# Delta-rule values and two gated branch outputs transposed on VectorE and through DRAM instead of on TensorE

## The chip, the cores and the metric

The kernel runs on one core of a Trainium2 chip. Its engines are TensorE (PE for its matmuls, PEld for its weight loads), VectorE (DVE), ScalarE (ACT), GpSimd (POOL) and SyncE (SP); each takes its own instructions in the order in which they were put into its queue. The metric is the device time of one execution in microseconds (us). A profiled execution gives the trace; its own time and its span (first to last instruction) are told beside the times of unprofiled runs.

## What is computed

One decoder layer on 256 tokens of width 2048, in float32. A token mixer adds three gated branches (multi-head latent attention, MLA; gated linear attention, GLA; gated DeltaNet, GDN); a convolutional gated MLP follows. What the change touches:

```python
h = rms_norm(x, attn_norm)
(..., gla_r, gdn_qkv, ..., gdn_z, merge) = split(h @ w_in)
# gated DeltaNet, chunks of the delta rule: 8 value heads of 128
v = silu(causal_dwconv(gdn_qkv, conv_w))[values]
u0 = triangular_solve(t_mat, beta * v)
...
y_gdn = rms_norm(o_gdn) * gain * silu(gdn_z)        # (256, 1024)
y_gla = rms_norm(o_gla) * gain * silu(gla_r)        # (256, 1024), 4 heads of 256
mixed = g_mla * (y_mla @ w_branch_mla) + g_gla * (y_gla @ w_branch_gla) + g_gdn * (y_gdn @ w_branch_gdn)
x = x + mixed @ w_out
x = x + conv_ffn(rms_norm(x))
return rms_norm(x, final_norm)
```

## The kernel before

Every large product keeps float32 accuracy by splitting both operands into a rounded high part and a low remainder. A weight piece of 128x1024 is loaded by SP (`raw`), rounded by ScalarE (`hi`, L191) and subtracted by VectorE (`lo`, whose operation shows as L103). There are four buffers each of `raw`, `hi` and `lo`, so a piece can be split ahead of its use. `t_chunk` (L237 to L239) gives 512 columns with tokens on the partitions, in matmuls of 128x512. `fj_chunk` (L212, L213) gives features on the partitions. Helpers record their own line: L103 is every elementwise product or sum, L106 every scalar-tensor-tensor operation, L293 the gain of `gained`.

A left operand of `t_chunk` must have features on the partitions. So a result with tokens on the partitions is transposed before it is a left operand again. There are two ways in the kernel. `gated_out` and V's scaling transpose 128x128 blocks on TensorE against an identity matrix, into PSUM. `turned` lets VectorE transpose inside 32x32 blocks (L304), writes the result to DRAM through POOL's queue (L306) and reads it back with the blocks in place, in four transfers per pair of 128-column blocks (L312); `gained_sb` then applies the gain and splits (ScalarE L323, VectorE L106). `turned` serves the merged sum and x + mixer, in three of their four chunks of 512 columns each.

The stages around the change, by the profile: the MLA branch until about 208 us; GDN's convolutions and gates until 265; its 31-step triangular solve on VectorE, 276 to 318, whose result POOL writes to DRAM and reads back (L759, L768); GDN's matmuls L796 to L832 until 435; GLA's projections q, k (an F chunk), V (`lv`, L944) and gate until 559; four GLA heads (L1026 and on) from 580 to 682. Merges (gate columns times branch product) and GDN's and GLA's projections lie between these on TensorE. `merge(0, y_mla)` fills the GDN stage; `merge(2, y_gdn, c)` is written after each GLA head; `merge(1, y_gla, c)` follows the heads.

Three places matter. V: `gv`, four tiles with two blocks of 128 features by 256 tokens each, is transposed at L781 (16 transposes) and multiplied by `vs` into `vt`, which L811 uses. GDN output: `gated_out` scales `o_gdn`, transposes (L865, 16) and splits into `hi_y` and `lo_y`. GLA output: the same function, 16 more transposes at L865, into `hi_E` and `lo_E`.

The order of each engine's queue is not written by hand: a planner simulates the program with its own costs for instructions and transfers, and takes what is ready by program order. An instruction can be tied behind the one written before it on its engine (`keep_in_program_order`). SBUF is handed out by tags with a fixed number of buffers (`S(tag)`); the tags of one region take the bytes of the region closed before it, tile by tile. In the GDN region those tags include "hq" (8 buffers) and "t" (4); in the GLA region "lqkv" (12), "E" (8) and "t" (4).

Of the kernel before, what the change touches and what calls it, by code (L numbers as in the profile page):

```python
# [9 lines left out]
F32 = mybir.dt.float32  # L10
# [3 lines left out]
AF = mybir.ActivationFunctionType  # L14
# [41 lines left out]
def trunk(ctx, tc, A, out, dbg=None, stop=None):  # L56
# [4 lines left out]
    def nm(s):  # L61
        serial[0] += 1
        return f"{s}{serial[0]}"
# [18 lines left out]
    def S(tag, shape=(P, 512), dt=F32, n=None):  # L82
        p, bufs = pools[tag]
        return p.tile(list(shape), dt, name=nm(n or tag), tag=tag, bufs=bufs)

    def PS(n="ps"):
        return pp.tile([P, 512], F32, name=nm(n), tag="mix")
# [7 lines left out]
    def keep(shape, n, dt=F32):  # L95
        return cp.tile(list(shape), dt, name=n)
# [5 lines left out]
    def tt(o, a, b, op, eng=None):  # L102
        (eng or dve).tensor_tensor(o, a, b, op=op)  # L103

    def stt(o, a, s, b, op0, op1):
        dve.scalar_tensor_tensor(o, a, s, b, op0=op0, op1=op1)  # L106
# [179 lines left out]
    def gained(psb, gains, store):  # L286

        hi, lo = store.new()
        if not isinstance(store, Joint):
            hi, lo = ([v[:, j] for j in range(2)] for v in (hi, lo))  # L290
        for j, g in enumerate(gains):
            src = psb[:, j * 256:(j + 1) * 256]
            act.activation(hi[j], src, AF.Copy, scale=g)  # L293
            stt(lo[j], src, g, hi[j], MUL, SUB)

    def turned(src, tags, n=512):

        nk = n // P  # L300
        d = dp.tile([2 * P, n], F32, name=nm("d_t"))
        for t in range(2):
            v = S(tags[0], (P, n), n="tr")
            dve.transpose(v.rearrange("p (b k i) -> p k b i", b=4, k=nk),  # L304
                          src[t].rearrange("p (k b i) -> p k b i", b=4, k=nk))
            pool.dma_start(d[t * P:(t + 1) * P], v)  # L306
        dv = d.rearrange("(a j) (b k i) -> b j a k i", j=32, b=4, k=nk)
        res = []
        for g in range(nk // 2):
            r = S(tags[1], (P, 8, 2, 32), n="rd")  # L310
            for b in range(4):
                pool.dma_start(r[b * 32:(b + 1) * 32], dv[b, :, :, 2 * g:2 * g + 2])  # L312
            res.append(r)
        return res

    def gained_sb(r, gains, store):

        hi, lo = store.new()
        if not isinstance(store, Joint):
            hi, lo = ([v[:, j] for j in range(2)] for v in (hi, lo))  # L320
        for j, g in enumerate(gains):
            h_, l_ = (v[j].rearrange("p (a i) -> p a i", i=32) for v in (hi, lo))
            act.activation(h_, r[:, :, j], AF.Copy, scale=g)  # L323
            stt(l_, r[:, :, j], g, h_, MUL, SUB)


    def row_stats(tiles, n):
# [307 lines left out]
        stt(gdec[:, t, :], xg[:, t, :], -1.0, ea, MUL, MUL)  # L635


    sel = keep([P, 68], "sel", F32R)
    pool.memset(sel.bitcast(F32), 0.0)
    pool.memset(sel[:, 3:4].bitcast(F32), 1.0)  # L640
# [133 lines left out]
    for gp in ((0, 1), (2, 3)):  # L774

        vts = {}
        for g in gp:
            psb = PS().rearrange("p (t x) -> p t x", t=2)
            for a in range(2):
                for t in range(2):  # L780
                    pe.transpose(psb[:, t, a * P:(a + 1) * P], gvv[2 * g + a][:, t * P:(t + 1) * P], ident)  # L781
            vts[g] = S("vt", (P, 2, 2, P))
            tt(vts[g].rearrange("p t a d -> p t (a d)"), psb, vs[:, :, g:g + 1].to_broadcast([P, 2, 256]), MUL)
        for s in (32, 64):
            work = []
            Pms = {g: S("Pm", (P, 4, s), n="Pm") for g in gp}
            for p in range(64 // s):
                for g in gp:
                    b1, b2 = slice(2 * p * s, 2 * p * s + s), slice(2 * p * s + s, 2 * p * s + 2 * s)
                    psb = PS()  # L790
                    pv = [psb[:, k * 128:k * 128 + 4 * s].rearrange("p (u j) -> p u j", u=4) for k in
                          ((0, 1, 2) if s == 32 else (0, 2))]
                    work.append((b1, b2, pv, Pms[g], Ms[g], Ys[g], Xs[g]))
            for b1, b2, pv, Pm, M, Y, X in work:
                for u in range(4):
                    pe.matmul(pv[0][b2, u, :], M[b1, u, b2], X[b1, u, b1], start=True, stop=True, **sk)  # L796
                dve.tensor_copy(Pm[b2], pv[0][b2])
            for b1, b2, pv, Pm, M, Y, X in work:
                for u in range(4):
                    pe.matmul(pv[1][b1, u, :], Pm[b2, u, :], Y[b2, u, b2], start=True, stop=True, **sk)  # L800
                dve.tensor_scalar(Y[b1, :, b2], pv[1][b1], -1.0, None, op0=MUL)
            if s == 32:
                for b1, b2, pv, Pm, M, Y, X in work:
                    for u in range(4):
                        pe.matmul(pv[2][b2, u, :], Y[b2, u, b2], Pm[b2, u, :], start=True, stop=True, **sk)
                    dve.tensor_scalar(X[b2, :, b1], pv[2][b2], -1.0, None, op0=MUL)
        u0s, W0s, R1s, W1s = {}, {}, {}, {}
        for g in gp:
            u0s[g] = PS()
            for a in range(2):  # L810
                pe.matmul(u0s[g][:, a * P:(a + 1) * P], Ys[g][:, a * 2, :], vts[g][:, 0, a, :], start=True, stop=True)  # L811
            W0s[g] = S("w", (P, 2, P), n="W0")
            tt(W0s[g], u0s[g][:, :256].rearrange("p (a d) -> p a d", a=2), b3(wj[:, 0, 2 * g:2 * g + 2], P), MUL)
        for g in gp:
            for a in range(2):
                pe.matmul(u0s[g][:, 256 + a * P:256 + (a + 1) * P], hqs[g][1][:, 1, a, :], W0s[g][:, a, :],
                          start=True, stop=True)
            R1s[g] = S("w", (P, 2, P), n="R1")
            tt(R1s[g], vts[g][:, 1], u0s[g][:, 256:].rearrange("p (a d) -> p a d", a=2), SUB)
        for g in gp:  # L820
            u1 = PS()
            for a in range(2):
                pe.matmul(u1[:, a * P:(a + 1) * P], Ys[g][:, a * 2 + 1, :], R1s[g][:, a, :], start=True, stop=True)
            W1s[g] = S("w", (P, 2, P), n="W1")
            tt(W1s[g], u1[:, :256].rearrange("p (a d) -> p a d", a=2), b3(wj[:, 1, 2 * g:2 * g + 2], P), MUL)
        for g in gp:
            op = PS().rearrange("p (t a d) -> p t a d", t=2, a=2)
            q0, q1 = hqs[g]
            for a in range(2):
                pe.matmul(op[:, 0, a, :], q0[:, 0, a, :], W0s[g][:, a, :], start=True, stop=True)  # L830
                pe.matmul(op[:, 1, a, :], q0[:, 1, a, :], W0s[g][:, a, :], start=True, stop=False)
                pe.matmul(op[:, 1, a, :], q1[:, 0, a, :], W1s[g][:, a, :], start=False, stop=True)  # L832
            os_ = S("d", (P, 2, 2, P), n="og")
            dve.tensor_copy(os_, op)
            o_gdn.append(os_)
            for a in range(2):
                for t in range(2):
                    junk = S("t", (P, P), n="junk")
                    c = t * 8 + 2 * g + a
                    act.activation(junk, os_[:, t, a, :], AF.Square, accum_out=gst[:, c:c + 1])  # L840
# [12 lines left out]
    for t in range(2):  # L853
        dve.tensor_scalar(fg[:, t, :], fg[:, t, :], rx[:, t:t + 1], None, op0=MUL)

    def gated_out(o_tiles, f_of, zs, gcol, name, ytag):

        y = Act(8, ytag)
        for g in range(4):
            o = o_tiles[g]  # L860
            f_of(g, o, [zs[t][g // 2][:, (g % 2) * 256:(g % 2) * 256 + 256] for t in range(2)])
            psb = PS()
            for a in range(2):
                for t in range(2):
                    pe.transpose(psb[:, a * 256 + t * P:a * 256 + (t + 1) * P], o[:, t, a, :], ident)  # L865
            gained(psb, [half_gain[:, gcol + 2 * g + a:gcol + 2 * g + a + 1] for a in range(2)], y)
            if dbg is not None and ("y_" + name) in dbg:
                full = S("t", (P, 2, 256), n="dbg")
                tt(full, y.hi[g].bitcast(F32), y.lo[g], ADD)
                sync.dma_start(dbg["y_" + name][:, 2 * g:2 * g + 2, :], full)  # L870
        return y

    def gates_of(c0, name, tag):
# [49 lines left out]
            tt(ov, ov, z[t], MUL)  # L923
        tt(o, o, fg[:, :, 2 * g:2 * g + 2].unsqueeze(3).to_broadcast([P, 2, 2, P]), MUL)

    y_gdn = gated_out(o_gdn, scale_gdn, zs, 8, "gdn", "y")
    if stop == "gdn":
        return

# [11 lines left out]
    for c in range(2):  # L941
        for t, bank in enumerate(t_chunk(w_in, GLA_V + c * 512, ht)):
            lv[t][c] = [S("lqkv", dt=F32R, n="lv") for _ in range(2)]
            act.activation(lv[t][c][0], bank, AF.Copy, scale=rx[:, t:t + 1])  # L944
            stt(lv[t][c][1], bank, rx[:, t:t + 1], lv[t][c][0], MUL, SUB)

    sr = gates_of(GLA_R, "rs", "d")


# [117 lines left out]
            ov = o[:, t].rearrange("p a d -> p (a d)")  # L1067
            stt(ov, ov, fl8[:, 2 * g + t:2 * g + t + 1], z[t], MUL, MUL)

    y_gla = gated_out(o_gla, scale_gla, sr, 0, "gla", "E")  # L1070
    if stop == "gla":
        return

# [206 lines left out]
```

## Time and profile before

| what | value |
|---|---|
| median of 3 runs | 1671.26 us (1670.92 to 1671.31) |
| profiled execution | 1671.5 us, span 1669.7 us, granted TensorE clock 0.998 |
| PE busy, PEld busy | 1656.2 us, 1406.8 us, 9068 instructions each |
| DVE busy | 1106.4 us, 1740 instructions |
| ACT busy | 828.0 us, 1157 instructions |
| POOL busy | 135.7 us, 202 instructions |
| DMA | 314.96 MB, mean 189 GB/s |

How to read it: busy times are the union of an engine's instructions, and since matmuls are pipelined, neighbours on PE overlap. The chain of waits starts at the last instruction and goes back, at each step to what released it or to the instruction before it on its engine. In a row of a group, `out<-in`, the shape and `xcount` come first, then the busy time, the mean of one and the idle time of the engine ahead of it with what ended it. A row of waits reads: who, for whom, us in all, times, longest. In a row of one line or tile, the three numbers are the shortest, middle and longest duration in ns, then the starts of the first and the last.

### The profile page before, as it was taken

The page shows a single profiled execution, that of the slowest core. Times are in us where ns is not written, and L with a number is a line of the kernel's source. Part 1 is how long each engine was busy: PE and PEld are TensorE (multiplying, and loading weights), DVE is VectorE, ACT ScalarE, POOL GpSimd, SP SyncE. Part 2 cuts the span into 40 slices and gives each one's busy share as a digit, 9 for nine tenths or more (in the row PEclk, how much of TensorE's full clock was granted, in tenths as well). Part 3 has the DMA queues.
Part 4 walks back from the last instruction along what each step waited for, and adds up shares of the span by engine and source line. Part 5 has one row for each costly group of instructions (what it writes and reads, how often), then busy time and mean ns, then how long its engine had stood idle before and what let it go on. Part 6 is the DMA issues. An engine that isn't in the chain of part 4 may idle for free.

```text
span 1669.7 us, 23887 instructions
## 1 busy us (share of the span) xinstructions
PE 1656.2 (99%) x9068; PEld 1406.8 (84%) x9068; DVE 1106.4 (66%) x1740; ACT 828.0 (50%) x1157; POOL 135.7 (8%) x202
## 2 busy tenths in 40 slices
PE   9999999999999999999999999999999999999997
PEld 7898888888888888888888888888888888888886
DVE  6868798755755795755656766664566665556666
ACT  6555563433444654444445654454355553345454
POOL 1000032200000000002112000000000000000000
PEclk9999999999999999999999999999999999999999
DMA  7565556654565456568777665656666566665653
GB/s 267 147 201 153 158 155 190 206 155 148 160 186 192 153 189 180 174 204 254 231 225 244 205 190 190 188 188 190 194 193 191 189 190 191 193 191 187 199 186 117
DMA packets 181059, 314.96 MB, mean 189 GB/s; under 512 B 17786, under 2 KB 45106, under 8 KB 180944
## 3 DMA queue, kind: packets, MB, share of 16 engines
q1 hardware_dynamic: 175488, 301.83, 57.7%
q0 software_dynamic: 5424, 11.60, 2.4%
q8 instruction: 71, 1.16, 0.3%
q14 instruction: 44, 0.36, 0.1%
q10 hardware_dynamic: 32, 0.01, 0.0%
HBM read 307.63 MB, written 5.77 MB: 188 GB/s over the span
## 4 chain that ended last, share of the span: by engine, by line
PE 94%; DVE 1%; issue 0%; ACT 0%; ACTq 0%
PE acc L239 17%; PE acc L237 17%; PE acc L238 17%; PE acc L212 15%; PE mix L212 10%; PE acc L213 8%; PE mix L213 5%; PE acc L1204 0%; PE acc L1206 0%; PE acc L1205 0%; PE ps L542 0%; PE ps L543 0%; DVE lo L103 0%; DVE u L103 0%; PE ps L1026 0%; PE ps L796 0%
## 5 line engine op out<-in xcount | busy, mean ns | idle before, releaser
L103 DVE TENSOR_TENSOR lo<-raw,hi 128x1024 fp32r<-128x1024 f32 (+2 forms) x571 | 686.6, 1205 | 498.9 <-ACT hi L191 496.1
L191 ACT CAST hi<-raw 128x1024 fp32r<-128x1024 f32 (+2 forms) x555 | 582.1, 1049 | 702.4 <-PE acc L239 412.2
L212 PE MATMUL acc<-hl_h,hi 128*128 128x512 f32 x1088 | 383.5, 397 | 0.0
L213 PE MATMUL acc<-hl_h,lo 128*128 128x256 f32 x1088 | 304.5, 280 | 0.0
L238 PE MATMUL acc<-lo,hl_h 128*128 128x512 f32 x640 | 249.3, 392 | 0.0
L239 PE MATMUL acc<-hi,hl_h 128*128 128x512 f32 x640 | 248.8, 392 | 0.0
L237 PE MATMUL acc<-hi,hl_h 128*128 128x512 f32 x640 | 247.4, 392 | 0.1
L212 PE MATMUL mix<-hl_h,hi 128*128 128x512 f32 x704 | 246.3, 395 | 0.0
L212 PEld LDWEIGHTS acc<-hl_h,hi 128*128 128x128 f32 x1088 | 203.9, 188 | 47.1
L213 PEld LDWEIGHTS acc<-hl_h,lo 128*128 128x128 f32 x1088 | 205.0, 188 | 1.0
L213 PE MATMUL mix<-hl_h,lo 128*128 128x256 f32 x704 | 196.0, 278 | 0.0
L212 PEld LDWEIGHTS mix<-hl_h,hi 128*128 128x128 f32 x704 | 132.1, 188 | 31.6
L237 PEld LDWEIGHTS acc<-hi,hl_h 128*128 128x128 f32 x640 | 120.3, 188 | 25.6 <-ACT hl_h L293 0.5
L238 PEld LDWEIGHTS acc<-lo,hl_h 128*128 128x128 f32 x640 | 120.5, 188 | 24.7
L239 PEld LDWEIGHTS acc<-hi,hl_h 128*128 128x128 f32 x640 | 120.3, 188 | 24.7
L213 PEld LDWEIGHTS mix<-hl_h,lo 128*128 128x128 f32 x704 | 132.5, 188 | 0.0
L238 PE MATMUL acc<-lo,hi_f 128*128 128x512 f32 x320 | 124.3, 389 | 0.0
L237 PE MATMUL acc<-hi,hi_f 128*128 128x512 f32 x320 | 124.2, 389 | 0.0
L239 PE MATMUL acc<-hi,lo_f 128*128 128x512 f32 x320 | 124.0, 389 | 0.0
L103 POOL TENSOR_TENSOR fcv<-fcv,rbc 128x512 f32<-128x512 f32 x22 | 31.3, 1424 | 669.0 <-ACT fcv L1161 669.0
L239 PEld LDWEIGHTS acc<-hi,lo_f 128*128 128x128 f32 x320 | 60.1, 188 | 12.5
L237 PEld LDWEIGHTS acc<-hi,hi_f 128*128 128x128 f32 x320 | 60.1, 188 | 12.5
(407 smaller groups left out, 1928.8 us busy)
## 6 DMA issues: line engine op xcount, KB each, us to landing
raw<-in_w_in_dram SPq DMA_DIRECT2D x207, 512.0 KB, 3.4
raw<-in_ffn_w_up_dram SPq DMA_DIRECT2D x176, 512.0 KB, 3.7
raw<-in_ffn_w_down_dram SPq DMA_DIRECT2D x88, 512.0 KB, 4.6
raw<-in_w_out_dram SPq DMA_DIRECT2D x32, 512.0 KB, 4.7
raw<-in_w_branch_mla_dram SPq DMA_DIRECT2D x16, 512.0 KB, 3.8
raw<-in_w_branch_gdn_dram SPq DMA_DIRECT2D x16, 512.0 KB, 3.8
raw<-in_w_branch_gla_dram SPq DMA_DIRECT2D x16, 512.0 KB, 6.1
raw<-in_mla_w_ukv_dram SPq DMA_DIRECT2D x8, 512.0 KB, 4.5
```

The source lines that it names most:

```text
L103: (eng or dve).tensor_tensor(o, a, b, op=op)
L191: act.copy(hi[:, ks], raw[:, ks])
L212: pe.matmul(banks[f], hi[:, kt, fs], joint[k], start=k == 0, stop=False, skip_group_check=True)
L213: pe.matmul(banks[f][:, :T], lo[:, kt, fs], joint[k][:, :T], start=False, stop=k == nk - 1, skip_group_check=True)
L237: pe.matmul(o, ah, hi[:, kt, :], start=first, stop=False)
L238: pe.matmul(o, ah, lo[:, kt, :], start=False, stop=False)
L239: pe.matmul(o, al, hi[:, kt, :], start=False, stop=last)
```

## The change

`turned` is cut into `turn_out` (transpose and write to DRAM) and `turn_in` (read back), and used at the three places instead of TensorE.

V is turned right after the gates: VectorE transposes each `gv` tile inside 32x32 blocks, POOL writes it to DRAM (2048-byte runs). Ahead of the chunk matmuls POOL reads it back in four transfers per tile (512-byte runs) into a "t" buffer, and VectorE scales it into `vt` in two operations out of SBUF instead of one out of PSUM.

`gated_out` now scales, transposes and writes; `gated_in` reads back and splits with `gained_sb`. The read-backs are in 256-byte runs. GDN's transposed tiles lie in "hq" buffers and its read-backs in "E" buffers. `gated_in` for GDN is written after GLA's V chunk, and its ScalarE and VectorE operations are tied in that order. GLA's go through "lqkv" buffers both ways, with no tie.

```diff
+    def turn_out(src, tag, n=512):
         nk = n // P
         d = dp.tile([2 * P, n], F32, name=nm("d_t"))
         for t in range(2):
+            v = S(tag, (P, n), n="tr")
             dve.transpose(v.rearrange("p (b k i) -> p k b i", b=4, k=nk),
                           src[t].rearrange("p (k b i) -> p k b i", b=4, k=nk))
             pool.dma_start(d[t * P:(t + 1) * P], v)
+        return d.rearrange("(a j) (b k i) -> b j a k i", j=32, b=4, k=nk)
+
+    def turn_in(dv, g, tag):
+        r = S(tag, (P, 8, 2, 32), n="rd")
+        for b in range(4):
+            pool.dma_start(r[b * 32:(b + 1) * 32], dv[b, :, :, 2 * g:2 * g + 2])
+        return r
+
+    def turned(src, tags, n=512):
+        dv = turn_out(src, tags[0], n)
+        return [turn_in(dv, g, tags[1]) for g in range(n // 256)]
...
-    def gained_sb(r, gains, store):
+    def gained_sb(r, gains, store, pin=False):
+        at = tc.keep_in_program_order if pin else lambda ins: ins
...
-            act.activation(h_, r[:, :, j], AF.Copy, scale=g)
-            stt(l_, r[:, :, j], g, h_, MUL, SUB)
+            at(act.activation(h_, r[:, :, j], AF.Copy, scale=g))
+            at(dve.scalar_tensor_tensor(l_, r[:, :, j], g, h_, op0=MUL, op1=SUB))
...
+    d_v = []
+    for g in range(4):
+        v = S("t", (P, 4, 4, 32), n="tr")
+        dve.transpose(v.rearrange("p b k i -> p k b i"), gv[g].rearrange("p a (t b i) -> p (a t) b i", t=2, b=4))
+        d = dp.tile([P, 4, 4, 32], F32, name=nm("d_v"))
+        pool.dma_start(d, v)
+        d_v.append(d.rearrange("(a j) b k i -> b j a k i", j=32))
...
         for g in gp:
-            psb = PS().rearrange("p (t x) -> p t x", t=2)
-            for a in range(2):
-                for t in range(2):
-                    pe.transpose(psb[:, t, a * P:(a + 1) * P], gvv[2 * g + a][:, t * P:(t + 1) * P], ident)
+            r = S("t", (P, 4, 2, 2, 32), n="rd")
+            for b in range(4):
+                pool.dma_start(r[b * 32:(b + 1) * 32].rearrange("p c a t i -> p c (a t) i"), d_v[g][b])
             vts[g] = S("vt", (P, 2, 2, P))
-            tt(vts[g].rearrange("p t a d -> p t (a d)"), psb, vs[:, :, g:g + 1].to_broadcast([P, 2, 256]), MUL)
+            for t in range(2):
+                dve.tensor_scalar(vts[g][:, t].rearrange("p a (c i) -> p a c i", i=32),
+                                  r[:, :, :, t].rearrange("p c a i -> p a c i"), vs[:, t, g:g + 1], None, op0=MUL)
...
-    def gated_out(o_tiles, f_of, zs, gcol, name, ytag):
-        y = Act(8, ytag)
+    def gated_out(o_tiles, f_of, zs, tag):
+        res = []
         for g in range(4):
             o = o_tiles[g]
             f_of(g, o, [zs[t][g // 2][:, (g % 2) * 256:(g % 2) * 256 + 256] for t in range(2)])
-            psb = PS()
-            for a in range(2):
-                for t in range(2):
-                    pe.transpose(psb[:, a * 256 + t * P:a * 256 + (t + 1) * P], o[:, t, a, :], ident)
-            gained(psb, [half_gain[:, gcol + 2 * g + a:gcol + 2 * g + a + 1] for a in range(2)], y)
+            res.append(turn_out([o[:, t].rearrange("p a d -> p (a d)") for t in range(2)], tag, 256))
+        return res
+
+    def gated_in(dvs, gcol, ytag, tag, pin=False):
+        y = Act(8, ytag)
+        for g in range(4):
+            gained_sb(turn_in(dvs[g], 0, tag),
+                      [half_gain[:, gcol + 2 * g + a:gcol + 2 * g + a + 1] for a in range(2)], y, pin)
         return y
...
-    y_gdn = gated_out(o_gdn, scale_gdn, zs, 8, "gdn", "y")
+    d_gdn = gated_out(o_gdn, scale_gdn, zs, "hq")
...
+    y_gdn = gated_in(d_gdn, 8, "y", "E", pin=True)
     sr = gates_of(GLA_R, "rs", "d")
...
-    y_gla = gated_out(o_gla, scale_gla, sr, 0, "gla", "E")
+    y_gla = gated_in(gated_out(o_gla, scale_gla, sr, "lqkv"), 0, "E", "lqkv")
```

More of the change, by code (lines that the diff above doesn't have):

```diff
@@ L294, in gained @@
             stt(lo[j], src, g, hi[j], MUL, SUB)
-    def turned(src, tags, n=512):
+    def turn_out(src, tag, n=512):
         nk = n // P
@@ L302, in turned @@
         for t in range(2):
-            v = S(tags[0], (P, n), n="tr")
+            v = S(tag, (P, n), n="tr")
             dve.transpose(v.rearrange("p (b k i) -> p k b i", b=4, k=nk),
@@ L306, in turned @@
             pool.dma_start(d[t * P:(t + 1) * P], v)
[L307 to L314, printed above, removed]
-    def gained_sb(r, gains, store):
+        return d.rearrange("(a j) (b k i) -> b j a k i", j=32, b=4, k=nk)
[9 more added lines that the diff above has]
+        at = tc.keep_in_program_order if pin else lambda ins: ins
         hi, lo = store.new()
@@ L861, in gated_out @@
             f_of(g, o, [zs[t][g // 2][:, (g % 2) * 256:(g % 2) * 256 + 256] for t in range(2)])
-            psb = PS()
-            for a in range(2):
-                for t in range(2):
-                    pe.transpose(psb[:, a * 256 + t * P:a * 256 + (t + 1) * P], o[:, t, a, :], ident)
-            gained(psb, [half_gain[:, gcol + 2 * g + a:gcol + 2 * g + a + 1] for a in range(2)], y)
[L867 to L870, printed above, removed]
+            res.append(turn_out([o[:, t].rearrange("p a d -> p (a d)") for t in range(2)], tag, 256))
[5 more added lines that the diff above has]
+                      [half_gain[:, gcol + 2 * g + a:gcol + 2 * g + a + 1] for a in range(2)], y, pin)
         return y
```

## The prediction, made before the changed kernel was run

> **What bounds the kernel now.** I read the page first (span, engine shares, shares of the chain), then TensorE's own waits, then the chain of waits around the three places that the change touches.
>
> ```profile
> span 1669.7 us, 23887 instructions
> ...
> PE 1656.2 (99%) x9068; PEld 1406.8 (84%) x9068; DVE 1106.4 (66%) x1740; ACT 828.0 (50%) x1157; POOL 135.7 (8%) x202
> ...
> PE 94%; DVE 1%; issue 0%; ACT 0%; ACTq 0%
> ```
>
> TensorE (PE) is busy for 99% of the span and carries 94% of the chain; POOL, which will issue every new transfer, is busy for 8%. A busy PE row can still hide starvation, so the next view asks what TensorE ever waited for (all its rows), and then what ScalarE's weight splits wait for:
>
> ```profile
> PE acc L1204 <- ACT hi_f L266: 1.1, 1, 1.1
> PE warm L159 <- DVE ones L155: 1.1, 1, 1.1
> PE ps L364 <- DMA x<-in_x_dram: 0.9, 1, 0.9
> PE acc L198 <- DVE lo L103: 0.5, 2, 0.4
> ```
> ```profile
> ACT hi L191 <- PE acc L239: 412.2, 252, 3.6
> ```
>
> TensorE waits 3.6 us in all, none of it in the stages that change. The splits of the weights (L191, L184) wait 412.2 us for TensorE to hand buffers back: the producers run ahead of TensorE, not behind it. So the time is TensorE's queue, and an instruction taken out of that queue gives back its pitch in it, as long as the producers stay ahead.
>
> **Part 1, what is taken off TensorE.** The change removes 48 transposes: 16 for V (L781), 16 for the DeltaNet output and 16 for the GLA output (both L865). The chain of waits lists the groups:
>
> ```profile
> 265.55 0.87 PE ps L781 x8
> ...
> 384.74 0.44 PE ps L781 x4
> ...
> 389.07 0.44 PE ps L781 x4
> ...
> 454.54 1.75 PE ps L865 x16
> ...
> 577.17 0.45 PE acc L237 x2
> ...
> 697.41 0.33 PE ps L865 x3
> ...
> 705.51 1.42 PE ps L865 x13
> ```
> ```profile
> L865 PE MATMUL ps<-ident,og x16: 271/272/273, 454.4 to 456.0; 128*128 128x128 f32 x16
> ```
>
> All six groups lie on the chain: 0.87 + 0.44 + 0.44 + 1.75 + 0.33 + 1.42 = 5.25 us, or 0.109 us for each of 48. I take this pitch and not the 0.272 us of the instruction's own row, because neighbours overlap: 16 of them start between 454.4 and 456.0.
> [...]
> What could be gained beyond 5.25 us are the seams where a group meets the weight matmuls; I bound them by one 512-wide matmul (0.45/2 = 0.23 us) for each of six groups, 1.4 us. Take: -5.25 us; bounds -6.65 and, with nothing to hide behind, -5.25 plus what follows.
>
> **Part 2, what is added on VectorE (DVE), ScalarE (ACT) and POOL.** The mechanism already runs in this kernel for six chunks of 512 columns (three of the merged sum, three of x + mixer), so its prices are rows:
>
> ```profile
> L304 DVE STREAM_TRANSPOSE tr<-mix x6: 666/685/703, 742.7 to 808.6; 128x512 f32<-128x512 f32 x6
> ```
> ```profile
> L306 POOL DMA_DIRECT2D d_t<-tr x12: 544/552/580, 743.7 to 906.0; - x12
> ...
> DMA to landing us min/median/max: 3.3/4.0/6.2
> ```
> ```profile
> L312 POOL DMA_DIRECT2D rd<-d_t x48: 582/583/612, 751.6 to 915.1; - x48
> ...
> DMA to landing us min/median/max: 3.2/5.0/6.3
> ```
> ```profile
> L103 DVE TENSOR_TENSOR vt<-ps,vs x4: 681/686/692, 266.0 to 389.9; 128x512 f32<-128x512 f32 x4
> ```
> ```profile
> L103 DVE TENSOR_TENSOR og<-og,zs x8: 415/421/425, 392.0 to 439.1; 128x256 f32<-128x256 f32 x8
> ...
> L103 DVE TENSOR_TENSOR og<-og,fg x4: 682/683/684, 449.7 to 451.5; 128x512 f32<-128x512 f32 x4
> ```
>
> V: four block transposes of 128x512 (4 x 0.69 = 2.7 us) and eight scalings of 128x256 in place of four products of 128x512 out of PSUM (4 x 0.69). No row shows that scaling; its bounds are 0 and the 0.42 us of the 128x256 product, and I take 0.42: +2.7 + 3.4 - 2.7 = +3.4 us. Each gated output: eight block transposes of 128x256, not shown, between 0.42 (the 128x256 product) and 0.69 (the 128x512 transpose); work goes by columns in these rows, so 0.42: +3.4 us each. The splits stay 8 + 8 per output, with SBUF in place of PSUM as source. Sum: about 10 us more on a VectorE that idles 563 us. POOL gets 4 + 8 + 8 writes at 0.55 and 3 x 16 reads at 0.58, 39 us in all. The traffic is three 1 MB trips each way, 6 MB. SP's queue, which brings all weights, gets nothing.
>
> **Part 3, what hides it, stage by stage.**
>
> ```profile
> 220.00:240.00 20.00, 20.00 (x92) 16.09 (x91) 17.72 (x35) 13.45 (x22) 5.58 (x4) 1.00 0.55 166
> ...
> 440.00:460.00 20.00, 20.00 (x121) 17.53 (x120) 18.23 (x40) 10.28 (x17) 0.00 (x0) 1.00 0.62 185
> ...
> 500.00:520.00 20.00, 20.00 (x89) 16.53 (x89) 10.95 (x10) 8.64 (x9) 0.00 (x0) 1.00 0.59 190
> ...
> 580.00:600.00 20.00, 20.00 (x191) 16.23 (x189) 20.00 (x66) 12.77 (x17) 0.00 (x0) 1.00 0.60 183
> ...
> 680.00:700.00 20.00, 20.00 (x95) 16.66 (x95) 13.59 (x29) 9.60 (x14) 0.00 (x0) 1.00 0.58 176
> ...
> 740.00:760.00 20.00, 20.00 (x90) 16.57 (x89) 12.07 (x15) 8.70 (x10) 6.78 (x12) 1.00 0.84 262
> ```
>
> The columns after the width are PE, PEld, DVE, ACT, POOL, clock, DMA share and GB/s.
>
> ```profile
> 319.12 1.07 POOL L759 DMA_DIRECT2D d_y<-xt  x2 [47.49 <-DVE xt L103]
> ...
> 331.77 2.17 POOL L768 DMA_DIRECT2D Y<-d_y  x4 [0.29 <-POOL Y L765]
> ...
> 436.26 0.44 POOL L1020 MEMSET aT<- 128x384 f32 x1
> ```
> ```profile
> 608.73 2.08 POOL L1042 COPY aT<-dia 32x64 f32<-32x64 f32 x4 [172.03 <-DVE dia L1035]
> ...
> 743.69 0.54 POOL L306 DMA_DIRECT2D d_t<-tr  x1 [68.52 <-DVE tr L304]
> ```
> ```profile
> L811 PE MATMUL ps<-vt,Y x16: 270/275/377, 363.6 to 420.6; 128*128 128x128 f32 x16
> ```
> ```profile
> L944 ACT ACTIVATE lv<-acc,rx x4: 690/690/690, 492.1 to 515.2; 128x512 fp32r<-128x512 f32 x4
> ```
> ```profile
> L106 DVE SCALAR_TENSOR_TENSOR ol<-ol,rsy,rs x8: 480/483/486, 688.8 to 691.6; 128x256 f32<-128x256 f32 x8
> ```
> ```profile
> L237 PE MATMUL acc<-hi,hi_E x64: 389/389/389, 728.6 to 836.7; 128*128 128x512 f32 x64
> ```
>
> V: the transposes lengthen VectorE's load near 230 (17.72 of 20) by 2.7 us, mostly in its 2.3 us of idle. The reads need the four "t" buffers that the 31-step solve also uses, so I expect them after it: POOL sends the solve's result at 319.12 and fetches Y until 333.9. Behind that, eight reads (4.7 us) land by 334 + 4.7 + 6.3 = 345, ahead of the first use of vt at 363.6. Put before Y instead, they make Y and the inverse 4.7 us later; TensorE has merge and GLA projections queued meanwhile. Price 0; without that cover, 4.7 us.
>
> DeltaNet output: eight splits on each engine leave the stage around 455 (VectorE 18.23 of 20), eight transposes come in: VectorE there changes by 3.4 - 8 x 0.48 = -0.4 us. The trip: scaling ends near 452, writes issue by 457 and land by 463, 16 reads issue by 473 and land by 479. The splits are pinned behind V's last chunk (515.2), so ScalarE finds bytes there and does not stand; behind them in both queues are weight splits, in a stage with VectorE at 10.95 and ScalarE at 8.64 of 20. The V chunk needs the "hq" bytes at 492, 29 us after the last write landed. POOL is idle from 436.7 to 608.73. Price 0; without cover, 8 x 0.48 = 3.8 us.
>
> GLA output: scaling ends at 692, eight transposes end near 697 with weight splits between them, the writes land near 703, 16 reads (9.3 us) issue by 713 and land by 719; POOL has nothing else until 743.69. The first product with y_GLA starts at 728.6: 9 us of slack for the last pair, more for the first. Price 0.
>
> DMA load: 740 to 760 already holds the same writes and reads beside the x loads, with the DMA share at 0.84 and TensorE at 20.00. Price 0, up to the 39 us of POOL if some engine stood for them.
>
> **The sum.** 1671.5 (the profiled execution's own time, span 1669.7) - 5.25 = 1666.25 us. That execution is 0.24 us above the median of the three runs (1671.26), so 1666.1 stands for both: -0.31%. A run must differ by about 0.2% (3.3 us) to be told from no change.
>
> **The rivals.**
> *The cover is thin somewhere and part comes back (about 1669.4, same).* In 580 to 600 VectorE has no idle time (20.00). If the planner's new order puts 3 us of the added work there (one output's transposes), TensorE waits for about that: -5.25 + 3.4 = -1.9. Against it: the pin keeps the DeltaNet splits at 515, and GLA's transposes need all four heads. Close to it: ScalarE already stands for read-backs:
>
> ```profile
> ACT hl_h L323 <- DMA rd<-d_t: 7.1, 4, 2.8
> ```
>
> Four such waits of up to 2.8 us cost TensorE nothing, but they show that the planner takes transfers as quicker than they are. Two of them on TensorE itself, at L811, would return 5.6 us (1671.6).
>
> *An in-order wait on V's bytes (about 1680, slower).* A scaling of V put into VectorE's queue before its read has landed holds every weight split behind it. A read lands in up to 6.3 us and 2.8 us of standing is known to be harmless, so each of the four V groups can cost 3.5 us: 14 - 5.25 = +8.8. It decides from 8.6 us of TensorE waits on. For it: the solve, the reads and vt share one queue and four buffers. Against it: 29 us between Y's last read and L811.
>
> *Weight loads come late behind the short runs (about 1676.4, slower).* The gated outputs are read back in runs of 256 bytes, eight groups of them. If each held one weight load by what separates the slowest read-back from the median one (6.3 - 5.0 = 1.3 us), with no lead left to cover it: 8 x 1.3 - 5.25 = +5.2. Against it: 740 to 760, where the same runs share the engines with weights and x and TensorE stays at 20.00.
> [...]
>
> *The transposes were not worth their pitch (1671.3, same).* If other work fills those slots at the same price, nothing is gained. Against it: the groups follow one another without idle, 99% busy.
>
> *Each is worth its whole 0.272 us (48 x 0.272 = 13.1, so 1658.2, faster).* Against it: the 1.75 us for 16.
> [...]
>
> **How the numbers follow.** Forecast 0.68 (1664.6 to 1667.8), part returned 0.16, not worth their pitch 0.04, in-order wait 0.08, late weights 0.02, whole durations 0.02. Faster by over 0.2% is 0.68 + 0.02 and 0.02 of the part returned, 0.72; slower 0.08 + 0.02 = 0.10; the rest, 0.18, is same. The low end is 1671.26 - 6.65 = 1664.6; the high end takes in the 1669.4 of the first rival with 0.8 us more, 1670.2.
>
> **What would show it.** Right: L781 and L865 gone, 48 TensorE instructions fewer, TensorE still at 20.00 in every 20 us window from 200 to 800, its waits still near 3.6 us, first hi_E product some 5 us earlier. Wrong: TensorE waits at L811, on hi_y or hi_E; VectorE idle before vt on rd; ScalarE idle on rd ahead of weight splits by more than 3 us; or a stage in which the same matmuls take longer.

## The result: 0.7% slower, and the profile after

| | before | after |
|---|---|---|
| median of 6 runs each | 1671.22 us | 1683.49 us (1681.7 to 1683.64) |
| ratio, 95% interval | | 1.0073 [1.0064, 1.0083] |
| profiled execution, span | 1671.5, 1669.7 us | 1681.7, 1679.9 us |

The change costs 12.3 us by the medians, where a gain of 5.2 was forecast. The profiled execution of the changed kernel is 1.8 us below its median, so the trace has 10.2 us to explain. The page of the changed kernel:

```profile
span 1679.9 us, 23955 instructions
...
PE 1651.4 (98%) x9020; PEld 1401.8 (83%) x9020; DVE 1113.8 (66%) x1764; ACT 827.4 (49%) x1157; POOL 173.7 (10%) x270
...
PE 91%; issue 3%; DVE 1%; POOL 0%; ACT 0%; DMA 0%; ACTq 0%; DVEq 0%; POOLq 0%
```

TensorE did lose its 48 instructions (9068 to 9020) and 4.8 us of busy time, yet the span grew, by time in which it stands. TensorE's waits name one long wait, in their first row, and the 20 us windows (columns as in the prediction) show the place. All other windows from 200 to 800 us have TensorE at 20.00, as before.

```profile
PE acc L212 <- DVE lq L103: 14.4, 1, 14.4
```
```profile
440.00:460.00 20.00, 5.64 (x40) 5.05 (x39) 14.25 (x42) 4.59 (x21) 5.75 (x11) 0.73 0.38 126
460.00:480.00 20.00, 20.00 (x110) 17.47 (x109) 10.16 (x12) 6.95 (x8) 10.85 (x20) 0.93 0.67 186
```

One wait of 14.4 us: GLA's next projection needs PSUM banks (`acc`) that still hold sums of `lq`, its q projection, and VectorE has not yet added them to `lq`. The first row shows a second loss, a granted clock of 0.73. Slices of 2 us of the same trace:

```profile
446.00:448.00 2.00, 0.00 (x0) 0.00 (x0) 2.00 (x6) 1.97 (x13) 0.00 (x0) 1.00 0.06 8
448.00:450.00 2.00, 0.00 (x0) 0.00 (x0) 1.76 (x11) 0.66 (x3) 0.00 (x0) 0.78 0.90 248
...
458.00:460.00 2.00, 0.63 (x2) 0.53 (x3) 1.39 (x5) 0.00 (x0) 2.00 (x5) 0.50 0.49 197
460.00:462.00 2.00, 2.00 (x8) 1.71 (x7) 1.51 (x3) 0.00 (x0) 2.00 (x4) 0.50 0.52 129
462.00:464.00 2.00, 2.00 (x11) 1.76 (x10) 0.00 (x0) 0.00 (x0) 2.00 (x5) 0.81 0.48 113
464.00:466.00 2.00, 2.00 (x13) 1.72 (x12) 0.00 (x0) 0.15 (x1) 2.00 (x4) 1.00 0.49 113
```

The clock falls to 0.50 some 4 us into the idle time and stays there for more than 3 us after the restart. Slices of 8 and 11 matmuls, where undisturbed ones hold 13 or 14, are some 8 matmuls short at 0.15 us each: about 1.2 us. The 0.63 us ahead of 460 hold 2 where 4 would stand, 0.3 us more. Then -5.25 + 14.4 + 1.5 = +10.7, by this estimate, against +10.2 in the spans.

Why `lq` is late shows in VectorE's order of time, after first, then before:

```profile
451.11 2.49 DVE L103 TENSOR_TENSOR og<-og,fg 128x512 f32<-128x512 f32 x4
453.52 2.72 DVE L302 STREAM_TRANSPOSE tr<-og 128x256 f32<-128x256 f32 x8
458.58 0.28 DVE L965 COPY glr<-few 16x256 f32<-16x256 f32 x1 [2.34 <-DMA d_t<-tr]
458.90 1.41 DVE L103 TENSOR_TENSOR lq<-lq,acc 128x256 f32<-128x256 f32 x4
```
```profile
439.10 0.42 DVE L103 TENSOR_TENSOR og<-og,zs 128x256 f32<-128x256 f32 x1
439.53 0.28 DVE L951 COPY glr<-few 16x256 f32<-16x256 f32 x1
439.85 0.75 DVE L103 TENSOR_TENSOR lq<-lq,acc 128x256 f32<-128x256 f32 x2
...
449.71 2.49 DVE L103 TENSOR_TENSOR og<-og,fg 128x512 f32<-128x512 f32 x4
```

Before, the first two sums of `lq` stood right behind the gating of the outputs (`og<-og,zs`), ahead of most of the root chain (a row of 0.17 us steps that make the reciprocal square roots), and all four ahead of the gain (`og<-og,fg`). After, all four stand behind the chain, the gain (451.11), the eight transposes (453.52) and a small copy into `glr`, which waits 2.34 us for the write of a transposed tile to land; by that wait, `glr` takes over bytes of such a tile.

And the stage itself is late. The first three fences are of the changed kernel: ScalarE's first squares of q, the last DeltaNet matmuls, and POOL's transfers behind the solve. The last two are the squares and the matmuls before; POOL's row before, `d_y` at 319.12, stands in the prediction.

```profile
L657 ACT ACTIVATE sq<-gq x2: 623/628/634, 226.1 to 230.5; 128x512 fp32r<-128x512 f32 x2
```
```profile
444.62 0.39 PE L845 MATMUL ps<-W,hq 128*128 128x128 f32 x2
```
```profile
332.50 4.37 POOL L792 DMA_DIRECT2D rd<-d_v  x8 [47.38 <-DVE el L103]
336.86 1.12 POOL L771 DMA_DIRECT2D d_y<-xt  x2
```
```profile
L645 ACT ACTIVATE sq<-gq x2: 630/632/634, 208.7 to 211.3; 128x512 fp32r<-128x512 f32 x2
```
```profile
434.49 0.39 PE L832 MATMUL ps<-W,hq 128*128 128x128 f32 x2
```

The squares use "t" buffers, and V's transposed tiles, written ahead of them, now take all four: the squares come only when the last `gv` has been made and is being transposed (226.06), 17 us later. POOL then reads eight pieces of V (4.37 us) ahead of the solve's result `d_y`, which leaves at 336.86 instead of 319.12. The stage ends 10 us later.

**Theory A**, from these rows and still to be shown: what the trips carry costs nothing; what costs is the order that their buffers bring. (1) V's tiles in "t" and V's reads ahead of `d_y` make the stage late. (2) The planner gives out the GLA stage's tiles only behind the last tile of the DeltaNet stage; with the transposed outputs in "hq" that tile comes after the gain, so the sums of `lq` (GLA tiles) go behind it. The rivals stand in the expectations, each with what it says there. The most obvious one is that the trips themselves cost it, by their bytes and their latency.

### The profile page after: what moved, and what is told of

Its sections match the earlier page's. It is cut to its first block, busy times and chain, and to the rows that moved or that the text cites. A ratio compares the mean times of both kernels' runs of the same rounds, so it can differ in the third digit from the quotient of the medians.

```text
span 1679.9 us, 23955 instructions
## 1 busy us (share of the span) xinstructions
PE 1651.4 (98%) x9020; PEld 1401.8 (83%) x9020; DVE 1113.8 (66%) x1764; ACT 827.4 (49%) x1157; POOL 173.7 (10%) x270
## 4 chain that ended last, share of the span: by engine, by line
PE 91%; issue 3%; DVE 1%; POOL 0%; ACT 0%; DMA 0%; ACTq 0%; DVEq 0%; POOLq 0%
PE acc L238 16%; PE acc L237 16%; PE acc L239 16%; PE acc L212 14%; PE mix L212 10%; PE acc L213 7%; PE mix L213 5%; PE acc L1218 0%; PE acc L1220 0%; PE acc L1219 0%; PE ps L545 0%; PE ps L546 0%; DVE lo L103 0%; DVE u L103 0%; PE ps L1040 0%
## 5 line engine op out<-in xcount | busy, mean ns | idle before, releaser
L212 PE MATMUL acc<-hl_h,hi 128*128 128x512 f32 x1088 | 385.0, 398 | 14.4 <-DVE lq L103 14.4
```

Of the source, the lines that this page charges most:

```text
L212: pe.matmul(banks[f], hi[:, kt, fs], joint[k], start=k == 0, stop=False, skip_group_check=True)
```

## Experiments: one part at a time

Each kernel is the changed one with two of the three trips put back on TensorE, or one:

```diff
 no_v:     V's d_v block, reads and two scalings out; 16 transposes and the 128x512 product in
 only_v:   both gated outputs as before the change
 only_gdn: V and GLA output as before the change
 only_gla: V and DeltaNet output as before the change
```

> The changed kernel with V back on TensorE (16 transposes at the old place); both gated outputs still go through DRAM. In the changed kernel TensorE stood for 14.4 us at L212 until VectorE summed lq, and the DeltaNet stage ended at 444.7 instead of 434.9. Theory A (two links: V's trip makes the DeltaNet stage late, and the DeltaNet output's trip puts its transposes ahead of the lq sums in VectorE's queue): the stage ends near 435 again, lq is summed some 14 to 18 us after that (449 to 453), TensorE runs out at about 447, so it stands 2 to 6 us: 1671.2 - 3.5 + 2 to 6 = 1670 to 1674 us. Theory B (the output's trip alone): about 14 us of standing remain, 1682 us. Theory C (V's trip alone): no standing, 1667.7 us.

> The kernel before with V's trip alone; both gated outputs on TensorE. Theory A: the DeltaNet stage ends near 444.7, lq is summed right after its last squares, near 449, TensorE runs out at 443: 6 us of standing, 1671.2 - 1.75 + 6 = about 1676 us. Theory B (the output's trip alone): no standing, 1669.5 us. Theory C (V's trip alone): the whole 14 us, 1684 us.

> The kernel before with the DeltaNet output's trip alone. Theory A: 1671.2 - 1.75 + 2 to 6 us of standing = 1671.5 to 1675.5 us, with the stage's end near 435. Theory B: about 1684 us. Theory C: 1669.5 us.

> The kernel before with the GLA output's trip alone. All three theories: the trip is hidden, 16 transposes of 0.109 us go: 1669.5 us (-0.10%).

| kernel | median, us | ratio to before (1671.26) | TensorE's wait for `lq` |
|---|---|---|---|
| no_v | 1679.27 | 1.0051 [1.0038, 1.0063] | 9.9 us |
| only_v | 1675.62 | 1.0029 [1.0018, 1.0039] | 4.1 us |
| only_gdn | 1680.95 | 1.0058 [1.0046, 1.0071] | 10.1 us |
| only_gla | 1669.86 | 0.9992 [0.9983, 1.0001] | none |

The top rows of TensorE's waits, of only_v, only_gdn and only_gla in this order:

```profile
PE acc L212 <- DVE lq L103: 4.1, 1, 4.1
```
```profile
PE acc L212 <- DVE lq L103: 10.1, 1, 10.1
```
```profile
PE acc L1224 <- ACT hi_f L266: 1.1, 1, 1.1
```

The parts add up: +4.4 (V) + 9.7 (DeltaNet) - 1.4 (GLA) = +12.7, against +12.3 for all. GLA's trip gives what 16 transposes are worth (1.75), within its interval, which also takes in no change. V's trip alone came out at theory A's time, near 1676, but not by its terms: TensorE waited 4.1 us where A had 6, and the slower clock behind the wait (granted 0.50 from 450 to 452 us and 0.69 from 452 to 454) made up most of the rest. For the DeltaNet output no theory's number held: only_gdn and no_v lie above A's (1671.5 to 1675.5, and 1670 to 1674) and below B's (1684 and 1682). A had sized this part too small: it had the sums at 449 to 453 (no_v's expectation), and in only_gdn's trace the gain in full (445.3 to 447.1) and the transposes (447.7 to 451.2) stand ahead of them, so that they start at 455.5; in no_v's, where the same stands ahead, `glr` waits 3.39 us in between for a write to land. That it is the order and not the trip had still to be shown.

## Experiments: the same trips in other buffers

```diff
 tr_in_d (after, DeltaNet output only, where tag is "hq"): one tile for both halves, from the main pool
-            v = S(tag, (P, n), n="tr")
     ...
+        v2 = S("d", (P, 2, n), n="tr")
     ...
 no_v_tr_in_d: the same in no_v
 v_in_g_pin (after, V only):
-        v = S("t", (P, 4, 4, 32), n="tr")
+        v = S("g", (P, 4, 4, 32), n="tr")
-                pool.dma_start(r[b * 32:(b + 1) * 32]..., d_v[g][b])
+                tc.keep_in_program_order(pool.dma_start(r[b * 32:(b + 1) * 32]..., d_v[g][b]))
 best_pin_d: tr_in_d and v_in_g_pin
```

> The changed kernel, with only the DeltaNet outputs' transposed tiles moved from the stage's own buffers (tag hq) to the main pool's tag d. Theory A (the planner hands the GLA stage's buffers out only behind the DeltaNet stage's last tile, so the outputs' gain, their transposes and a wait for a landing write stand ahead of the lq sums in VectorE's queue): the lq sums stand ahead of the eight transposes again, no wait for the write d_t is left in front of them, TensorE's wait for the lq banks falls from 14.4 us to the 4 us that V's turn alone gave, and the time to 1670 to 1672.5 us against 1671.3 before. Rival B (the trips themselves cost it, wherever their buffers lie: bytes, issue, latency): the wait stays near 14 us and the time near 1683 us.

> The same with V's turn on TensorE as before: 32 of 48 transposes are gone. Theory A: no wait for the lq banks over 1 us, and 32 x 0.109 = 3.5 us less than before: 1667 to 1668.5 us. Rival B: the 10 us wait of the kernel with both outputs turned stays, 1679 us. Rival D (the queue's pitch is not what a removed transpose returns): no wait, but 1670.5 to 1671.5 us.

> The changed kernel, with V's transposed tiles in tag g instead of t and the reads of V's bytes pinned in program order behind the inverse's (d_y out, the four Y in, then V). The outputs' turn is as in the changed kernel. Theory A: the DeltaNet stage is on time again (its last matmul near 435 to 438 us against 444.7), and what is left is the outputs' part, a wait of about 10 us: 1676.5 to 1678.5 us. Rival E (V's lateness is the trip's own latency, not who holds the t buffers and who stands first in the queue): the last matmul stays near 444 us and the time near 1683 us.

> Both mendings at once: V's transposed tiles in g with the reads pinned, the outputs' transposed tiles in d. Theory A: no wait for the lq banks over 1 us, all 48 transposes gone at 0.109 us each: 1665.5 to 1667 us, 4 to 6 us faster than before. Rival B: 1679 to 1683 us. Rival D: 1670.5 to 1671.5 us.

| kernel | median, us | ratio to before (1670.77) | wait for `lq` |
|---|---|---|---|
| tr_in_d | 1672.91 | 1.0011 [1.0002, 1.002] | 4.1 us |
| no_v_tr_in_d | 1668.75 | 0.9987 [0.9978, 0.9996] | none |
| v_in_g_pin | 1678.11 | 1.004 [1.0028, 1.0053] | 11.0 us |
| best_pin_d | 1665.59 | 0.9967 [0.9954, 0.9979] | none |

The three trips move the same bytes in tr_in_d and the changed kernel. What differs is the tag of the DeltaNet output's transposed tiles, and that both halves share a tile. VectorE's order in tr_in_d:

```profile
449.09 0.28 DVE L978 COPY glr<-few 16x256 f32<-16x256 f32 x1
449.40 0.42 DVE L103 TENSOR_TENSOR lq<-lq,acc 128x256 f32<-128x256 f32 x1
...
454.66 2.50 DVE L103 TENSOR_TENSOR og<-og,fg 128x512 f32<-128x512 f32 x4
457.08 2.72 DVE L314 STREAM_TRANSPOSE tr<-og 128x256 f32<-128x256 f32 x8
```

`lq` is back ahead of the gain and the copy into `glr` waits for nothing: 14.4 us of wait fall to 4.1, and the time by 10.6 us. The median is 0.4 us above what A gave as its upper end. After the restart the clock stands at half for longer than in the changed kernel (7, 8 and 11 matmuls in the slices from 450 to 456, some 14 short, 2.1 us). That is not the whole of it: -5.25 + 4.1 + 2.1 gives +1.0, the medians +2.1, and the rest stays open.

```profile
446.00:448.00 2.00, 0.00 (x0) 0.00 (x0) 2.00 (x4) 2.00 (x15) 1.64 (x4) 0.97 0.19 44
448.00:450.00 2.00, 0.12 (x1) 0.12 (x1) 1.96 (x8) 1.41 (x6) 0.00 (x0) 0.50 0.66 158
450.00:452.00 2.00, 2.00 (x7) 1.71 (x8) 2.00 (x7) 0.00 (x0) 0.00 (x0) 0.50 0.46 163
452.00:454.00 2.00, 2.00 (x8) 1.71 (x8) 1.73 (x10) 0.00 (x0) 0.00 (x0) 0.50 0.00 0
454.00:456.00 2.00, 2.00 (x11) 1.74 (x11) 1.90 (x7) 0.00 (x0) 0.00 (x0) 0.82 0.00 0
```

With V on time as well (best_pin_d), nothing of the loss is left. POOL sends the solve's result and Y first, V behind them; TensorE's longest wait is the 1.1 us that it had before; the window of the stall is full:

```profile
324.77 1.08 POOL L783 DMA_DIRECT2D d_y<-xt  x2 [48.50 <-DVE xt L103]
...
340.20 3.79 POOL L804 DMA_DIRECT2D rd<-d_v  x7
```
```profile
PE acc L1231 <- ACT hi_f L266: 1.1, 1, 1.1
```
```profile
440.00:460.00 20.00, 20.00 (x116) 17.39 (x116) 19.44 (x43) 8.98 (x13) 6.00 (x11) 1.00 0.66 187
```

1665.59 - 1670.77 = -5.2 us, the 48 x 0.109 of the prediction (interval -7.7 to -3.5). This version beats both kernels. So the trips themselves cost nothing that can be seen here, and a transpose less on TensorE is worth about its pitch (5.2 / 48 = 0.108 us, against 0.109). no_v_tr_in_d, at 2.0 us below before with 3.5 expected, is just above A's range, and its interval (-3.7 to -0.7) takes in A's number. v_in_g_pin shows that V is the smaller half: with the stage on time the wait is still 11.0 us.

## Experiments: which part of each

```diff
 g_only_d:   best_pin_d without the tie on V's reads
 pin_only_d: best_pin_d with V's transposed tiles left in "t"
 glr_late (after):
-    glr = S("glr", (81, T))
-    dve.tensor_copy(glr[64:80, :], few[64:80, :])
     ...
     y_gdn = gated_in(d_gdn, 8, "y", "E", pin=True)
+    glr = S("glr", (81, T))
+    tc.keep_in_program_order(dve.tensor_copy(glr[64:80, :], few[64:80, :]))
 hold_only (before the change):
     y_gdn = gated_out(o_gdn, scale_gdn, zs, 8, "gdn", "y")
+    hold = S("hq", (P, 2, 2, P), n="hold")
+    dve.tensor_copy(hold[:, 0, 0, 0:32], o_gdn[3][:, 0, 0, 0:32])
```

> The doubly mended kernel without the pin: V's transposed tiles in g, the outputs' in d, but the planner free to put the reads of V's bytes ahead of the inverse's write d_y in POOL's queue. Which of V's two faults costs what: if the late t buffers are the whole of it, the DeltaNet stage ends near 436 us and the time stays at the doubly mended kernel's 1665.6 (1665 to 1667). If the eight reads in front of d_y count too, the stage ends 4 us later, near 440, TensorE waits up to 2 us for the lq banks, and the time is 1667 to 1669.5 us. Rival B (bytes and latency of the trips) is out by now and expects nothing else here.

> The other half: V's transposed tiles left in t (the keys' squares wait for them), the reads pinned behind the inverse's, the outputs' tiles in d. If the t buffers are V's main fault, the squares start at 226 us as in the changed kernel, d_y goes out near 332.5 and the stage ends near 440 us: a wait of 0 to 3 us at the lq banks and 1667 to 1671 us. If the order in POOL's queue is, the stage ends near 436 us and the time is 1665 to 1667 us.

> The changed kernel, with the copy into glr (the one instruction that waits for a landing write ahead of the lq sums) moved behind the outputs' gain splits and nothing else. If that landing wait is a part of the stall of its own, TensorE's wait falls by its 2.3 us from 14.4 to about 12 us and the time to 1680.5 to 1681.5 us; if the lq sums are held by the gain and the transposes alone, or by the next thing behind them, nothing moves: 1683 us.

> The kernel before the change, all transposes on TensorE, with one copy of 128x32 added: behind the DeltaNet outputs' gain, out of the last output into a tile of tag hq that nobody reads. No trip, no transfer, 0.2 us of VectorE. Theory A (a last tile of the DeltaNet stage that ends late holds back every tile of the next stage): the lq sums go behind the root chain and the gain in VectorE's queue, TensorE waits 4 to 8 us for the lq banks near 447 us, and the time is 1676 to 1681 us. Rival F (the stage's tiles are not handed out that way, and it was the trip's own instructions that stood in front): no wait over 1 us and 1671 to 1671.5 us.

| kernel | median, us | ratio to before (1671.02; hold_only: 1670.9) | wait for `lq` |
|---|---|---|---|
| g_only_d | 1667.36 | 0.9978 [0.9969, 0.9987] | none |
| pin_only_d | 1667.33 | 0.998 [0.9971, 0.9989] | none |
| glr_late | 1680.01 | 1.0055 [1.0041, 1.0068] | 11.6 us |
| hold_only | 1677.94 | 1.0042 [1.0029, 1.0056] | 3.7 us |

V first. The tie alone (tiles in "t") has its squares at 226 us and its last DeltaNet matmul at 438.4; the other buffers alone have the squares at 208.4, but POOL reading V for 4.36 us ahead of `d_y`, and the last matmul at 439.2; both together 435.9, none 445.4 (tr_in_d). The time in the table does not order the two, and neither makes TensorE wait. Mending either one brings the stage forward by 6 or 7 us, and with `lq` in its old place that is enough for TensorE not to wait. That they end 1.7 us above best_pin_d without such a wait is not explained. The intervals overlap, and the profiled spans are 1665.7 and 1664.8 us against 1663.3 there.

`glr_late` takes one instruction out of the way: wait -2.8 us, time -3.5 against the changed kernel's 1683.49, both a little more than was expected. The landing write is a part of its own of the 14.4 us, about a fifth.

hold_only shows (2) without any trip. The kernel before the change plus one copy of 0.17 us, whose result nobody reads, is 7.0 us slower:

```profile
PE acc L212 <- DVE lq L103: 3.7, 1, 3.7
```
```profile
445.29 2.49 DVE L103 TENSOR_TENSOR og<-og,fg 128x512 f32<-128x512 f32 x4
...
449.62 0.17 DVE L928 COPY hold<-og 128x32 f32<-128x32 f32 x1
...
450.60 0.41 DVE L953 COPY glr<-few 16x256 f32<-16x256 f32 x1
...
451.83 1.41 DVE L103 TENSOR_TENSOR lq<-lq,acc 128x256 f32<-128x256 f32 x4
```

The order is turned round as in the changed kernel, gain first and `lq` last. How the planner hands out tiles is inferred from such orders: with another tag (tr_in_d) `lq` goes back to the front, with one late tile added (hold_only) it goes to the back. The wait (3.7 us) is a little under the range given; the time, inside it. Its profiled execution has a span of 1674.8 us, 5.1 over before's, which the 3.7 us of wait and a clock of 0.91 in that window make up; its median runs are longer, and what they have more is not seen in this one trace.

## Why the prediction was wrong, by its own steps

**Part 1, -5.25 us: right in kind, its size not settled to the tenth.** best_pin_d returns 5.2 us for the 48. But g_only_d and pin_only_d return 3.7 us for the same 48, and no_v_tr_in_d 2.0 us for 32, so how close 5.2 comes is in part luck. The rival of 0.272 us each (1658.2) lies outside best_pin_d's interval. The 0.272 us of the row is the duration of one, with its neighbours overlapping (16 of them take 1.75 us on the chain).

**Part 2, prices on VectorE and POOL: right.** The 128x256 transposes took 0.40 us (taken: 0.42), V's scalings 0.35 us (0.42). POOL grew by 38.0 us (39).

**Part 3, V: failed.** Two steps of it. "The reads need the four "t" buffers that the 31-step solve also uses, so I expect them after it" looked at the readers of "t" but not at the new writers: the transposed tiles take the same four buffers, in front of the squares, and these start 17 us late. The other case, reads ahead of Y, was named, and priced at 0 because "TensorE has merge and GLA projections queued meanwhile". That cover was true in kind and too thin: both faults together end the stage 10 us later, and TensorE stood 4.1 us for it. Price 0 measured as 6.1 us (only_v: +4.4, and the 1.75 that 16 transposes fewer should have given).

**Part 3, DeltaNet output: failed, and this is the larger term.** "VectorE there changes by 3.4 - 8 x 0.48 = -0.4 us" compared sums of work in a window. What decided was who stands ahead of whom in VectorE's queue. The step asked when the "hq" bytes would be wanted by the V chunk at 492 us; `glr`, `lq` and the rest of the GLA stage's tiles were wanted from 439 on, and all of them come behind the last DeltaNet tile. Price 0 measured as 11.4 us (only_gdn: +9.7, and the 1.75 again).

**Part 3, GLA output and DMA load: right.** only_gla lost nothing. In best_pin_d TensorE stays at 20.00 beside both outputs' read-backs. ScalarE's waits for the read-backs of `hl_h`, the row that the prediction showed, rose in the changed kernel from 7.1 to 13.0 us, the longest to 5.9, and TensorE's waits show none of them.

**The rivals.** The one on the slower side (an in-order wait on V's bytes, 1680, given 0.08) had the sign and the kind: VectorE's queue holding, in order, other things in front of what TensorE needs. That its 1680 comes near 1683 is luck. It looked for it at `vt`, where VectorE waited 2.4 us in all and TensorE not at all. It was at `lq`, a tile that the change does not touch. No wait of TensorE for late weights is longer than 0.4 us, and the VectorE windows at 20.00 (580 to 620 us in the changed kernel) cost nothing: TensorE is at 20.00 in both.

## What to carry over

Before a new tile is given a tag, list everything that takes buffers of that tag behind it, and everything that takes its bytes when the region closes: a tile that ends late holds all of that back, even with 0.17 us of work in it. Cover must be read as an order of instructions on the queue of each engine, with the next result that TensorE needs marked in it, not as busy shares of a window. When a change that should be hidden is not, put the same work into other buffers first: here two tags and a tie turned +12.3 us into -5.2.

## What was not expected of the hardware

In two runs a stall cost more than its length. An idle time of 4.1 us (tr_in_d) was followed by a granted clock of 0.50, and so was one of 14.4 us (changed kernel): by the short slices some 2.1 and 1.5 us on top, so that the longer stall cost no more of this than the shorter. When the clock changed differs between the two. In the changed kernel's trace, slices of 0.1 us have it at 1.00 up to 449.1 and at 0.51, then 0.50, from there on: it fell some 4.1 us into an idle time that began near 445.0. They have it at 0.50 up to 462.7, at 0.73 to 462.8 and at 1.00 from there on: it came back some 3.4 us behind the restart at 459.4. In the trace of tr_in_d, if the clock is either 1.00 or 0.50 there too, the 0.97 between 446 and 448 puts the fall some 2.1 us into an idle time that began near 445.8, and the 0.82 between 454 and 456 the return some 4.8 us behind the restart at 449.9. So these two traces show no fixed time for either.
